# A hybrid block on one core: projection groups in another order (recurrent and gate groups in turn, the first v/z group and the gates moved forward)

## The chip, the core and the metric

The kernel runs on one core of one Trainium2 chip. The metric is the device time of one execution in microseconds. Times of instructions and waits come from one profiled execution.

## The reference

One layer of a decoder trunk with three parallel head groups. 2048 tokens of width 1024 are normalised and projected once to 5656 columns, whose parts feed attention, a Mamba-2 mixer (SSD) and a gated linear recurrence (RG-LRU); each branch has a SiLU gate, and the three are mapped back by one output projection and added to the input.

```python
u = rms_norm(h, norm_g[l])
proj = jnp.einsum('bsd,de->bse', u, w_in[l])
(q, k, v, z_att, f_raw, z_ssd, xbc, dt_raw, x_lru, z_lru) = jnp.split(proj, split_points, axis=-1)
log_f = jax.nn.log_sigmoid(f_raw + forget_b[l])
y_att = fox_attention(q, k, v, log_f, q_norm_g[l], k_norm_g[l]) * jax.nn.silu(z_att)
y_ssd = ssd_mixer(xbc, dt_raw, z_ssd, ...)     # silu(conv(xbc)), softplus(dt_raw + bias), chunked scan, y * silu(z_ssd), norm
y_lru = rglru_mixer(x_lru, ...) * jax.nn.silu(z_lru)   # conv, two 64-wide gate products per block, scan over time
mix = jnp.concatenate([y_att, y_ssd, y_lru], axis=-1)
h = h + jnp.einsum('bse,ed->bsd', mix, w_out[l])
```

The widths are 512 each for q, k, v, z_att, x_lru and z_lru, 1024 for z_ssd, 1536 for xbc, 8 for f_raw, 16 for dt_raw. All is float32.

## The kernel before, in words

**Projection.** The normalised input, transposed, stays in SBUF as two float32r parts, `uh` and `ul` (four token blocks `tb` of 512, eight slices `k` of 128 channels). Each projection of 256 columns is a *group*. `weights` (L178 to L196) gets a group's columns: for each of eight slices k one load (issued by SP) into a raw tile `wr` (4 buffers), a ScalarE cast to `wh` (L192), and a subtraction `wl = wr − wh` (L193) on the engines of `eng` in turn: VectorE, or GpSimd for even and VectorE for odd k. `wh` and `wl` have eight buffers each, so a group's tile k takes the place of the previous group's tile k. A product is three matmuls per k: wh·uh, wh·ul and wl·uh. `proj_ch` (L347) puts channels on the partitions (128x512 matmuls, 24 to a tile), `proj_tok` (L315) and `proj_tok2` (L325) put tokens there (128x280 and 128x256); all take their PSUM from three banks, `psj`.

**Order.** The program text sets the order of the groups, and the scheduler interleaves the steps of neighbours:

1. the norm of x, block by block, with transposes by PE (`pu`, L293/L295). x comes in 16 tiles `xt` from a pool of XB = 8 buffers;
2. six convolution groups (L409 to L446, tiles `pxx`, `accx`): convolution on ACT (L397, L402) and DVE (L405), tanh on ACT (L431) and a product on DVE (L432), transposes on PE (L439), stores to `xs_d`, `b_d`, `bt_d`, `ct_d`;
3. the first v/z group, `group_vz(0)` (L358, tiles `pvz`): 128 columns of v, 128 of z_att and the 24 of f_raw and dt_raw; its evictions are two DVE operations and two small copies (L387, L388) a tile;
4. four recurrent groups m = 0 to 3 (L523 to L615, tiles `pll` and `pzl`): each 128 columns of x_lru and 128 of z_lru, with the convolution, the gate products on PE (`pgal`, `pgxl`, L583 to L585), exponentials, tanh and Sqrt on ACT, the reciprocal (L591), a scan over time (L607) and the last product (L611) on DVE, and products for z on POOL (L567, L568). The steps' order is the string LORD;
5. four z groups for the SSD branch (L618 to L630, tiles `pzs`): a tanh on ACT into a tile `thzs`, one DVE operation into `zs`, a store. The first of them takes two of its eight tiles from the bank pool `pst`. `gates` (L453, decays of both branches: softplus, exponentials, cumulative sums by small matmuls) comes ahead of the second (GM = 1);
6. the SSD stage, in which the groups of q and k (`pqk`) and the other v/z groups fill TensorE, then attention and the output projection.

Engines run their own queues in program order, so an instruction that waits holds all behind it on its engine.

Of the kernel before, what the change touches and what calls it, by code (L numbers as in the profile page):

```python
# [8 lines left out]
F32 = mybir.dt.float32  # L9
# [3 lines left out]
AF = mybir.ActivationFunctionType  # L13
ALU = mybir.AluOpType
# [4 lines left out]
P = 128  # L19
S = 2048  # L20
D = 1024
NT = S // P
KD = D // P
EPS = 1e-6
C_Q, C_K, C_V, C_ZA, C_F, C_ZS, C_X, C_DT, C_XL, C_ZL = (
    0, 512, 1024, 1536, 2048, 2056, 3080, 4616, 4632, 5144)
# [12 lines left out]
NDV = 3  # L39
UP, DOWN = (0, 1, 2, 3, 4, 5, 6, 7), (7, 6, 5, 4, 3, 2, 1, 0)  # L40
ORD = (DOWN,) + (UP,) * 6 + (DOWN,)
XB = 8
GM = 1
PB = (2, 3, 2, 1)


# [1 line left out]
def hybrid_block(ctx, tc, x, norm_g, w_in, q_norm_g, k_norm_g, forget_b, ssd_conv_w, ssd_conv_b,  # L48
# [3 lines left out]
    def tpool(**kw):  # L52
        if kw.get("space") is not DRAM:
            kw["reuse_waits"] = "tile"
        return tc.tile_pool(**kw)

    V, A, G, T = nc.vector, nc.scalar, nc.gpsimd, nc.tensor
    dma = nc.sync.dma_start
# [16 lines left out]
    xs_d = [dram(f"xs_d{g}", [S, 512]) for g in range(2)]  # L75
    b_d = [dram(f"b_d{g}", [S, P]) for g in range(2)]
# [13 lines left out]
    ident = ctile("ident", [P, P])  # L90
# [14 lines left out]
    CV = {}  # L105
# [28 lines left out]
    def softplus(pool, y, xin, shape, tag):  # L134
        def tmp(nm):
            return pool.tile(shape, F32, name=f"{tag}_{nm}", tag=f"sp_{nm}")
        ax, e, d, z2, p = tmp("a"), tmp("e"), tmp("d"), tmp("z"), tmp("p")
        V.scalar_tensor_tensor(ax, xin, -1.0, xin, op0=ALU.mult, op1=ALU.max)
        A.activation(e, ax, AF.Tanh, scale=1.0 / 16.0)
        V.tensor_scalar(d, e, 1.0, None, op0=ALU.add)  # L140
        V.reciprocal(d, d)
        V.tensor_scalar(e, e, -1.0, 1.0, op0=ALU.mult, op1=ALU.add)
        V.tensor_tensor(e, e, d, op=ALU.mult)
        for _ in range(3):
            V.tensor_tensor(e, e, e, op=ALU.mult)
        V.tensor_scalar(d, e, 2.0, None, op0=ALU.add)
        V.reciprocal(d, d)
        V.tensor_tensor(e, e, d, op=ALU.mult)
        V.tensor_tensor(z2, e, e, op=ALU.mult)
        V.tensor_scalar(p, z2, 1.0 / 19.0, None, op0=ALU.mult)  # L150
        for k in (17, 15, 13, 11, 9, 7, 5, 3):
            V.scalar_tensor_tensor(p, p, 1.0 / k, z2, op0=ALU.add, op1=ALU.mult)
        V.scalar_tensor_tensor(p, p, 1.0, e, op0=ALU.add, op1=ALU.mult)
        V.tensor_scalar(ax, xin, 0.0, None, op0=ALU.max)
        V.scalar_tensor_tensor(y, p, 2.0, ax, op0=ALU.mult, op1=ALU.add)
# [22 lines left out]
    def weights(cols, rawp=wrp, eng=(V,)):  # L178

        n = sum(w for _, w in cols)  # L180
        i = gcount[0]
        gcount[0] += 1
        wh, wl = [], []
        for k in range(KD):
            raw = rawp.tile([P, n], F32, name=f"wr{i}_{k}", tag="wr")
            h = wp.tile([P, n], F32R, name=f"wh{i}_{k}", tag="wh")
            l = wp.tile([P, n], F32R, name=f"wl{i}_{k}", tag="wl")
            o = 0
            for c, w in cols:
                dma(raw[:, o:o + w], w_in[k * P:(k + 1) * P, c:c + w])  # L190
                o += w
            A.copy(h, raw)  # L192
            eng[k % len(eng)].tensor_tensor(l, raw, h.bitcast(F32), op=ALU.subtract)  # L193
            wh.append(h)
            wl.append(l)
        return wh, wl, n  # L196

    rtx = ExitStack()
    rtp = rtx.enter_context(tpool(name="rtp", bufs=2, side="right"))
    cvp = rtx.enter_context(tpool(name="cvp", bufs=2, side="right"))  # L200
# [146 lines left out]
    def proj_ch(w, m, tb, name):  # L347
        wh, wl, n = w
        ps = psj.tile([P, 512], F32, name=name, tag="pj")
        ms = slice(m * P, m * P + P)  # L350
        for k in range(KD):
            T.matmul(ps, wh[k][:, ms], uh[tb][k], start=(k == 0), stop=False)  # L352
            T.matmul(ps, wh[k][:, ms], ul[tb][k], start=False, stop=False)  # L353
            T.matmul(ps, wl[k][:, ms], uh[tb][k], start=False, stop=(k == KD - 1))  # L354
        return ps
# [39 lines left out]
    def conv(pool, ps, prev, wname, bname, m, nm, ntile, acc, tag=""):  # L395
        rt = pool.tile([P, 515], F32, name=f"rt{nm}", tag="rt" + tag)
        A.copy(rt[:, 3:515], ps)  # L397
        if prev is None:
            G.memset(rt[:, 0:3], 0.0)
        else:  # L400
            G.tensor_copy(rt[:, 0:3], prev[:, 512:515])
        A.activation(acc, rt[:, 3:515], AF.Identity, scale=c1(wname, 3 * ntile + m),  # L402
                     bias=c1(bname, m))
        for k in range(3):
            V.scalar_tensor_tensor(acc, rt[:, k:k + 512], c1(wname, k * ntile + m), acc,  # L405
                                   op0=ALU.mult, op1=ALU.add)
        return rt

    g0x = ExitStack()  # L409
    g0 = g0x.enter_context(tpool(name="g0", bufs=2))  # L410
    with tpool(name="cl", bufs=1) as cl:
        for gq in range(6):
            if gq == 3:
                ll = cl.tile([P, 4], F32, name="ll")
                j = CV["lam"]
                V.tensor_scalar(ll, cv[:, j:j + 4], -1.0, None, op0=ALU.mult)
                softplus(cl, lsp, ll, [P, 4], "spl")
                V.tensor_scalar(lsp, lsp, 8.0, None, op0=ALU.mult)
                V.tensor_scalar(nlsp, lsp, -1.0, None, op0=ALU.mult)
            w = weights([(C_X + gq * 256, 256)]) if gq else wx0  # L420
            prev = [None, None]
            for tb in range(4):
                for mm in range(2):
                    m = gq * 2 + mm
                    nm = f"x{m}_{tb}"
                    ps = proj_ch(w, mm, tb, f"px{nm}")
                    acc = cv3.tile([P, 512], F32, name=f"acc{nm}", tag="acc")
                    prev[mm] = conv(rtp, ps, prev[mm], "cw", "cb", m, nm, 12, acc, str(mm))

                    th = prev[mm][:, 0:512]  # L430
                    A.activation(th, acc, AF.Tanh)  # L431
                    V.scalar_tensor_tensor(acc, th, 1.0, acc, op0=ALU.add, op1=ALU.mult)  # L432
                    ts = slice(tb * 512, tb * 512 + 512)
                    if m >= 8:
                        dma((bt_d if m < 10 else ct_d)[m % 2][:, ts], acc)
                    if m < 10:
                        pt = pst.tile([P, 4, P], F32, name=f"ptx{nm}", tag="pt")
                        for i in range(4):
                            T.transpose(pt[:, i, :], acc[:, i * P:(i + 1) * P], ident)  # L439
                        st = cvp.tile([P, 4, P], F32, name=f"st{nm}", tag="stx")  # L440
                        A.copy(st, pt)
                        if m < 8:
                            dst = xs_d[m // 4][ts, (m % 4) * P:(m % 4 + 1) * P]
                        else:
                            dst = b_d[m - 8][ts, :]
                        dma(dst.rearrange("(i p) c -> p i c", p=P), st)  # L446

    rtx.close()
    sgx = ExitStack()
    sg = sgx.enter_context(tpool(name="sg", bufs=1, side="right"))  # L450
    nacs, eacs, dec = (sg.tile([P, NT, 16], F32, name=nm) for nm in ("nacs", "eacs", "dec"))

    def gates(g1):  # L453

        dtb = g1.tile([P, 16], F32, name="dtb")
# [60 lines left out]
        for t in range(NT):  # L516
            dma(c_d[:, t, :], cr[t * 8:(t + 1) * 8, :])

    group_vz(g0, g0, 0)
    g0x.close()  # L520


    with tpool(name="lxs", bufs=2) as lxs, tpool(name="lp1", bufs=1) as lp1, tpool(name="lp", bufs=2) as pool:  # L523
        wbd = {}
        HB = 1024
        for m in range(4):
# [86 lines left out]

            for st in LORD.split():
                {"x": stage_x, "z": stage_z, "g": stage_g}[st[0]](int(st[1]))  # L615


    with tpool(name="zp", bufs=2, side="right") as pool, tpool(name="g1", bufs=1, side="right") as g1:  # L618
        for gq in range(4):
            if gq == GM:  # L620
                gates(g1)
            w = weights([(C_ZS + gq * 256, 256)], eng=(G, V) if gq < 2 else (V,))
            for t2 in range(8):
                zt = pool.tile([P, 2, 256], F32, name=f"zs{gq}_{t2}", tag="zs")
                ps = proj_tok2(w, t2, f"pzs{gq}_{t2}", (pst, "pt") if t2 % 5 > 2 and gq == 0 else None)
                th = pool.tile([P, 2, 256], F32, name=f"thzs{gq}_{t2}", tag="thzs")
                A.activation(th, ps, AF.Tanh, scale=0.5)
                V.scalar_tensor_tensor(zt, th, 1.0, ps, op0=ALU.add, op1=ALU.mult)
                dst = zs_d[gq // 2][t2 * 256:(t2 + 1) * 256, (gq % 2) * 256:(gq % 2 + 1) * 256]
                dma(dst.rearrange("(i p) c -> p i c", p=P), zt)  # L630

    sx = ExitStack()
    s1 = sx.enter_context(tpool(name="s1", bufs=1, side="right"))
# [478 lines left out]
```

## Time and profile before

| | us |
|---|---|
| median of 3 runs (2066.79 to 2068.64) | 2068.15 |
| the profiled execution | 2066.93 |
| its span | 2065.2 |
| PE busy | 2000.1 |
| DVE busy | 1268.8 |
| ACT busy | 978.6 |
| POOL busy | 542.1 |

PE is TensorE's matmul, PEld its weight load, DVE VectorE, ACT ScalarE, POOL GpSimd, SP the queue that issues most DMAs. In a timeline a row is start, duration, engine, line, operation, output<-input, shape; in brackets stands how long the engine had been idle and what released it. A wait row has the engine and line that waited, what it waited for, the sum in us, how often, and the longest. Matmuls overlap: a 128x512 matmul is recorded as 0.39 us and the next starts 0.23 us behind it. The granted clock is TensorE's, as a share of full speed.

### The profile page before, as it was taken

To read this page: it belongs to the slowest core of one execution; us is meant where nothing else is said; L and a number is where in the kernel's file an instruction comes from. 1 tells how busy PE (TensorE), PEld (TensorE's weight loads), DVE (VectorE), ACT (ScalarE), POOL (GpSimd) and SP (SyncE) were. 2 spreads that over 40 slices of the span, in tenths; PEclk is the share of its full clock that TensorE was granted. 3 is DMA by queue.
4 is the path that set the end of the run, shared out by engine and by line. 5 is a ranking of instruction groups with operands and counts; after the bars stand their busy time and mean duration, and the time that the engine had idled before them with its cause. 6 is when DMAs were issued, how large, how long until landed. Compare 5 with 4: busy or idle time off the path is not lost. (4 is left out here: it accounts for less than half of the span.)

```text
span 2065.2 us, 36048 instructions
## 1 busy us (share of the span) xinstructions
PE 2000.1 (97%) x12517; PEld 1756.8 (85%) x12517; DVE 1268.8 (61%) x2684; ACT 978.6 (47%) x2049; POOL 542.1 (26%) x790
## 2 busy tenths in 40 slices
PE   7999999999999999989999999899998999999999
PEld 6788889887789999878888998788887888888887
DVE  6755553488885225768666255666776776875333
ACT  7644443466642114544444234566665666664110
POOL 0100000255531004455553001243333333323110
PEclk9999999999999999999999999999999999999999
DMA  5222232111123225657666746575476375443443
GB/s 195 59 72 67 77 98 81 44 43 43 42 62 103 69 75 152 200 174 211 200 165 181 194 128 200 145 194 160 135 192 171 112 189 163 121 131 89 137 142 118
DMA packets 287317, 265.18 MB, mean 128 GB/s; under 512 B 59780, under 2 KB 227232, under 8 KB 285088
## 3 DMA queue, kind: packets, MB, share of 16 engines
q1 hardware_dynamic: 286976, 262.85, 43.9%
q8 instruction: 99, 1.62, 0.3%
q0 software_dynamic: 160, 0.03, 0.1%
q14 instruction: 82, 0.67, 0.1%
HBM read 168.22 MB, written 94.57 MB: 127 GB/s over the span
## 5 line engine op out<-in xcount | busy, mean ns | idle before, releaser
L940 DVE TENSOR_TENSOR pl<-T,ph 128x512 fp32r<-128x512 f32 (+2 forms) x352 | 191.3, 565 | 71.7 <-ACT ph L939 70.2
L1002 PE MATMUL po<-woh,mh 128*128 128x512 f32 x512 | 213.0, 416 | 10.2 <-DVE xr L1010 5.3
L939 ACT CAST ph<-T 128x512 fp32r<-128x512 f32 (+2 forms) x352 | 161.9, 491 | 124.5 <-PE T L932 85.0
L1003 PE MATMUL po<-wol,mh 128*128 128x512 f32 x512 | 201.9, 394 | 0.0
L1004 PE MATMUL po<-woh,ml 128*128 128x512 f32 x512 | 200.8, 397 | 0.0
L932 PE MATMUL T<-ident,L 128*128 128x128 f32 x1088 | 171.6, 275 | 3.9 <-ACT L L882 2.8
L882 ACT ACTIVATE L<-L,mx 128x1920 f32<-128x1920 f32 (+15 forms) x128 | 154.5, 1208 | 41.1 <-DVE mx L879 36.7
L352 PE MATMUL pxx<-uh,wh 128*128 128x512 f32 x384 | 153.0, 402 | 3.4 <-ACT uh L297 3.4
L918 PE MATMUL O<-ph,vv 128*128 128x256 f32 x576 | 154.1, 288 | 0.6 <-ACT ph L939 0.5
L919 PE MATMUL O<-pl,vv 128*128 128x256 f32 x576 | 152.4, 289 | 0.4 <-DVE pl L940 0.3
L353 PE MATMUL pxx<-ul,wh 128*128 128x512 f32 x384 | 152.7, 401 | 0.0
L340 PE MATMUL pqk<-wh,ul 128*128 128x256 f32 x512 | 151.1, 295 | 0.0
L354 PE MATMUL pxx<-uh,wl 128*128 128x512 f32 x384 | 151.1, 396 | 0.0
L336 PE MATMUL pqk<-wh,uh 128*128 128x256 f32 x512 | 150.2, 294 | 0.0
L338 PE MATMUL pzs<-wl,uh 128*128 128x256 f32 x512 | 144.6, 283 | 2.8 <-POOL wl L193 2.8
L338 PE MATMUL pqk<-wl,uh 128*128 128x256 f32 x512 | 145.9, 285 | 0.0
L336 PE MATMUL pzs<-wh,uh 128*128 128x256 f32 x512 | 144.6, 283 | 0.7 <-ACT wh L192 0.7
L405 DVE SCALAR_TENSOR_TENSOR accx<-rtx,cv,accx 128x512 f32<-128x512 f32 x144 | 108.2, 752 | 59.9 <-ACT accx L402 56.3
L340 PE MATMUL pzs<-wh,ul 128*128 128x256 f32 x512 | 144.2, 282 | 0.0
L932 PEld LDWEIGHTS T<-ident,L 128*128 128x128 f32 x1088 | 126.8, 141 | 15.2 <-ACT L L882 6.8
L871 POOL TENSOR_SCALAR_AFFINE_SELECT cm<-cb 128x384 f32<-128x384 f32 (+3 forms) x128 | 58.8, 462 | 300.9 <-DVE mx L879 146.2
L670 ACT ACTIVATE ab<-ab,nacs 128x128 f32<-128x128 f32 x256 | 82.2, 391 | 117.3 <-POOL ab L666 117.1
(319 smaller groups left out, 5605.6 us busy)
## 6 DMA issues: line engine op xcount, KB each, us to landing
ab<-acs_d SPq DMA_DIRECT2D x64, 256.0 KB
pt_d<-xr SPq DMA_DIRECT2D x64, 256.0 KB
wr<-in_w_in_dram SPq DMA_DIRECT2D x192, 64.0 KB
wr<-in_w_in_dram SPq DMA_DIRECT2D x80, 128.0 KB
xt<-in_x_dram SPq DMA_DIRECT2D x16, 512.0 KB
xs_d<-stx SPq DMA_DIRECT2D x32, 256.0 KB
v_d<-vs SPq DMA_DIRECT2D x32, 256.0 KB
zs_d<-zs SPq DMA_DIRECT2D x32, 256.0 KB
```

What stands on the lines that cost most here:

```text
L336: T.matmul(ps[:, i, :], h[k][:, sl], wh[k], start=(k == 0 and i == 0), stop=False, skip_group_check=True)
L338: T.matmul(ps[:, i, :], h[k][:, sl], wl[k], start=False, stop=False, skip_group_check=True)
L340: ins = T.matmul(ps[:, i, :], l[k][:, sl], wh[k], start=False, stop=last, skip_group_check=True)
L352: T.matmul(ps, wh[k][:, ms], uh[tb][k], start=(k == 0), stop=False)
L882: A.activation(lt[:, 0:n], lt[:, 0:n], AF.Exp, bias=mx, scale=-1.0, accum_out=sm[:, i:i + 1])
L918: T.matmul(po[:, ca], vv[:, kt, :], ph[:, jj, ca], start=(kt == 0), stop=False)
L932: ins = T.transpose(pt[:, jj, i * P:(i + 1) * P], L[i][:, kt * P:(kt + 1) * P], ident)
L939: A.copy(ph[:, ja, ca], pt[:, ja, ca])
L940: V.tensor_tensor(pl[:, ja, ca], pt[:, ja, ca], ph[:, ja, ca].bitcast(F32), op=ALU.subtract)
L1002: T.matmul(ps, mh[:, j, :], h, start=(j == 0), stop=False)
L1003: T.matmul(ps, mh[:, j, :], l, start=False, stop=False)
L1004: T.matmul(ps, ml[:, j, :], h, start=False, stop=(j == 3))
```

## The change

The numbers are computed as before; the order of the groups is another, with what makes room for it:

- the pool of x tiles has 7 buffers instead of 8 (XB), the three tiles `nacs`, `eacs`, `dec` are allocated at the start, and `gates` gets its own tiles beside the convolutions;
- `group_vz(0)` is issued ahead of the second convolution group (gq = 1), `gates` ahead of the third (gq = 2);
- the z groups become a function `group_zs`, called behind each recurrent group, so that they run recurrent 0, z 0, recurrent 1, z 1, and so on. All four z groups split their `wl` between GpSimd and VectorE (before, the last two had VectorE alone), all tiles take their PSUM from `psj`, and the tanh is written into `zs` itself, in which DVE then works in place.

From the end of the last z group on, every engine has the same instructions in the same order.

```diff
-XB = 8
-GM = 1
+XB = 7
...
+    sgx = ExitStack()
+    sg = sgx.enter_context(tpool(name="sg", bufs=1, side="right"))
+    nacs, eacs, dec = (sg.tile([P, NT, 16], F32, name=nm) for nm in ("nacs", "eacs", "dec"))
...
-    with tpool(name="cl", bufs=1) as cl:
+    with tpool(name="cl", bufs=1) as cl, tpool(name="g1", bufs=1, side="right") as g1:
         for gq in range(6):
+            if gq == 1:
+                group_vz(g0, g0, 0)
+            if gq == 2:
+                gates(g1)
...
-    group_vz(g0, g0, 0)
     g0x.close()
+    zpx = ExitStack()
+    zp = zpx.enter_context(tpool(name="zp", bufs=2, side="right"))
+
+    def group_zs(gq):
+        w = weights([(C_ZS + gq * 256, 256)], eng=(G, V))
+        for t2 in range(8):
+            ps = proj_tok2(w, t2, f"pzs{gq}_{t2}")
+            zt = zp.tile([P, 2, 256], F32, name=f"zs{gq}_{t2}", tag="zs")
+            A.activation(zt, ps, AF.Tanh, scale=0.5)
+            V.scalar_tensor_tensor(zt, zt, 1.0, ps, op0=ALU.add, op1=ALU.mult)
+            dst = zs_d[gq // 2][t2 * 256:(t2 + 1) * 256, (gq % 2) * 256:(gq % 2 + 1) * 256]
+            dma(dst.rearrange("(i p) c -> p i c", p=P), zt)
...
             for st in LORD.split():
                 {"x": stage_x, "z": stage_z, "g": stage_g}[st[0]](int(st[1]))
...
-    with tpool(name="zp", bufs=2, side="right") as pool, tpool(name="g1", bufs=1, side="right") as g1:
-        for gq in range(4):
-            if gq == GM:
-                gates(g1)
-            w = weights([(C_ZS + gq * 256, 256)], eng=(G, V) if gq < 2 else (V,))
-            for t2 in range(8):
-                zt = pool.tile([P, 2, 256], F32, name=f"zs{gq}_{t2}", tag="zs")
-                ps = proj_tok2(w, t2, f"pzs{gq}_{t2}", (pst, "pt") if t2 % 5 > 2 and gq == 0 else None)
-                th = pool.tile([P, 2, 256], F32, name=f"thzs{gq}_{t2}", tag="thzs")
-                A.activation(th, ps, AF.Tanh, scale=0.5)
-                V.scalar_tensor_tensor(zt, th, 1.0, ps, op0=ALU.add, op1=ALU.mult)
-                dst = zs_d[gq // 2][t2 * 256:(t2 + 1) * 256, (gq % 2) * 256:(gq % 2 + 1) * 256]
-                dma(dst.rearrange("(i p) c -> p i c", p=P), zt)
+            if m < 3:
+                group_zs(m)
+    group_zs(3)
+    zpx.close()
```

On TensorE, the end of the first recurrent group (the last gate product, `pgxl0_2`) and what follows it; the numbers in a weight's name are the count of the group and the slice k. Before:

```order
L583 MATMUL pgxl0_2_4020<-xhl0_2_3853,bdhx0_3687 128x512
L584 MATMUL pgxl0_2_4020<-xhl0_2_3853,bdlx0_3688 128x512
L585 MATMUL pgxl0_2_4020<-xll0_2_3854,bdhx0_3687 128x512
L352 MATMUL pll1_0_4131<-uh0_0_147,wh8_0_4059 128x512
L353 MATMUL pll1_0_4131<-ul0_0_155,wh8_0_4059 128x512
L354 MATMUL pll1_0_4131<-uh0_0_147,wl8_0_4060 128x512
```

And in the changed kernel:

```order
L598 MATMUL pgxl0_2_4181<-xhl0_2_4014,bdhx0_3848 128x512
L599 MATMUL pgxl0_2_4181<-xhl0_2_4014,bdlx0_3849 128x512
L600 MATMUL pgxl0_2_4181<-xll0_2_4015,bdhx0_3848 128x512
L338 MATMUL pzs0_0_4267<-wh8_0_4220,uh0_0_147 128x256
L340 MATMUL pzs0_0_4267<-wl8_0_4221,uh0_0_147 128x256
L342 MATMUL pzs0_0_4267<-wh8_0_4220,ul0_0_155 128x256
```

The second recurrent group's first tile has given its place to the first z group's, which asks for its `wl` one matmul earlier.

On GpSimd, the end of the second recurrent group: the subtractions for the group that follows (`wl9` before, `wl10` in the changed kernel), the low part of the convolution's result (`xll`) and the products of the z columns (`tzl`, `ZZ`). Before:

```order
L193 TENSOR_TENSOR wl9_0_4495<-wr9_0_4493,wh9_0_4494 128x256
L554 TENSOR_TENSOR xll1_3_4382<-XC1_1_4255,xhl1_3_4381 128x512
L193 TENSOR_TENSOR wl9_2_4509<-wr9_2_4507,wh9_2_4508 128x256
L193 TENSOR_TENSOR wl9_4_4523<-wr9_4_4521,wh9_4_4522 128x256
L567 TENSOR_TENSOR tzl1_2_4411<-tzl1_2_4411,ZZ1_1_4385 128x512
L567 TENSOR_TENSOR tzl1_3_4441<-tzl1_3_4441,ZZ1_1_4385 128x512
L193 TENSOR_TENSOR wl9_6_4537<-wr9_6_4535,wh9_6_4536 128x256
L568 TENSOR_TENSOR ZZ1_1_4385<-tzl1_2_4411,ZZ1_1_4385 128x512
```

And in the changed kernel:

```order
L569 TENSOR_TENSOR xll1_3_5015<-XC1_1_4888,xhl1_3_5014 128x512
L192 TENSOR_TENSOR wl10_0_5128<-wr10_0_5126,wh10_0_5127 128x256
L192 TENSOR_TENSOR wl10_2_5140<-wr10_2_5138,wh10_2_5139 128x256
L192 TENSOR_TENSOR wl10_4_5152<-wr10_4_5150,wh10_4_5151 128x256
L192 TENSOR_TENSOR wl10_6_5164<-wr10_6_5162,wh10_6_5163 128x256
L582 TENSOR_TENSOR tzl1_2_5044<-tzl1_2_5044,ZZ1_1_5018 128x512
L582 TENSOR_TENSOR tzl1_3_5074<-tzl1_3_5074,ZZ1_1_5018 128x512
L583 TENSOR_TENSOR ZZ1_1_5018<-tzl1_2_5044,ZZ1_1_5018 128x512
```

The four subtractions stand together, behind `xll` and ahead of the z products; at the end of the first recurrent group they are mixed with them as before.

On SP, the loads of x behind the first weight tiles of the second group in the program's order (`wr1`: the second convolution group before, the v/z group with four pieces a tile in the changed kernel). Before:

```order
L239 DMA rows_298<-in_k_norm_g_dram 1x64
L240 DMA rows_298<-in_k_norm_g_dram 1x64
L190 DMA wr1_0_1041<-in_w_in_dram 128x256
L190 DMA wr1_1_1047<-in_w_in_dram 128x256
L208 DMA xt8_312<-in_x_dram 128x1024
L208 DMA xt9_314<-in_x_dram 128x1024
```

And in the changed kernel:

```order
L242 DMA rows_304<-in_k_norm_g_dram 1x64
L189 DMA wr1_0_1050<-in_w_in_dram 128x128 x2
L189 DMA wr1_0_1050<-in_w_in_dram 128x8
L210 DMA xt7_299<-in_x_dram 128x1024
L210 DMA xt8_318<-in_x_dram 128x1024
L210 DMA xt9_320<-in_x_dram 128x1024
```

The load of `xt7`, which before stood right behind `xt6`, now stands here, in front of `xt8`.

More of the change, by code (lines that the diff above doesn't have):

```diff
@@ L407, in conv @@
         return rt
-    g0x = ExitStack()
-    g0 = g0x.enter_context(tpool(name="g0", bufs=2))
-    with tpool(name="cl", bufs=1) as cl:
[L412 to L451, printed above, removed]
     def gates(g1):
@@ L517, in gates @@
             dma(c_d[:, t, :], cr[t * 8:(t + 1) * 8, :])
-    group_vz(g0, g0, 0)
-    g0x.close()
+    g0x = ExitStack()
+    g0 = g0x.enter_context(tpool(name="g0", bufs=2))
+    with tpool(name="cl", bufs=1) as cl, tpool(name="g1", bufs=1, side="right") as g1:
+        for gq in range(6):
+            if gq == 1:
+                group_vz(g0, g0, 0)
+            if gq == 2:
+                gates(g1)
+            if gq == 3:
+                ll = cl.tile([P, 4], F32, name="ll")
+                j = CV["lam"]
+                V.tensor_scalar(ll, cv[:, j:j + 4], -1.0, None, op0=ALU.mult)
+                softplus(cl, lsp, ll, [P, 4], "spl")
+                V.tensor_scalar(lsp, lsp, 8.0, None, op0=ALU.mult)
+                V.tensor_scalar(nlsp, lsp, -1.0, None, op0=ALU.mult)
+            w = weights([(C_X + gq * 256, 256)]) if gq else wx0
+            prev = [None, None]
+            for tb in range(4):
+                for mm in range(2):
+                    m = gq * 2 + mm
+                    nm = f"x{m}_{tb}"
+                    ps = proj_ch(w, mm, tb, f"px{nm}")
+                    acc = cv3.tile([P, 512], F32, name=f"acc{nm}", tag="acc")
+                    prev[mm] = conv(rtp, ps, prev[mm], "cw", "cb", m, nm, 12, acc, str(mm))
+                    th = prev[mm][:, 0:512]
+                    A.activation(th, acc, AF.Tanh)
+                    V.scalar_tensor_tensor(acc, th, 1.0, acc, op0=ALU.add, op1=ALU.mult)
+                    ts = slice(tb * 512, tb * 512 + 512)
+                    if m >= 8:
+                        dma((bt_d if m < 10 else ct_d)[m % 2][:, ts], acc)
+                    if m < 10:
+                        pt = pst.tile([P, 4, P], F32, name=f"ptx{nm}", tag="pt")
+                        for i in range(4):
+                            T.transpose(pt[:, i, :], acc[:, i * P:(i + 1) * P], ident)
+                        st = cvp.tile([P, 4, P], F32, name=f"st{nm}", tag="stx")
+                        A.copy(st, pt)
+                        if m < 8:
+                            dst = xs_d[m // 4][ts, (m % 4) * P:(m % 4 + 1) * P]
+                        else:
+                            dst = b_d[m - 8][ts, :]
+                        dma(dst.rearrange("(i p) c -> p i c", p=P), st)
```

1 line of the change is left out of this document (added).

## The prediction

> **What bounds the kernel now.** I read the page's busy shares first, then busy time by stretches of 50 us, then TensorE's waits. All times below are of the profiled execution: it took 2066.93 us, its span is 2065.2 us.
>
> ```profile
> PE 2000.1 (97%) x12517; PEld 1756.8 (85%) x12517; DVE 1268.8 (61%) x2684; ACT 978.6 (47%) x2049; POOL 542.1 (26%) x790
> ```
>
> ```profile
> 50.00:100.00 50.00, 48.23 (x253) 39.38 (x252) 39.43 (x94) 31.56 (x58) 5.50 (x15) 1.00 0.20 55
> 100.00:150.00 50.00, 50.00 (x239) 40.84 (x238) 29.67 (x45) 25.26 (x45) 1.31 (x8) 1.00 0.26 74
> 300.00:350.00 50.00, 48.86 (x302) 44.39 (x301) 23.36 (x60) 17.08 (x39) 0.60 (x4) 1.00 0.28 78
> 350.00:400.00 50.00, 50.00 (x298) 44.84 (x297) 17.35 (x45) 14.85 (x37) 9.08 (x11) 1.00 0.22 61
> 400.00:450.00 50.00, 50.00 (x218) 40.46 (x217) 43.01 (x41) 32.58 (x51) 24.09 (x23) 1.00 0.16 44
> 450.00:500.00 50.00, 47.49 (x203) 37.53 (x202) 43.18 (x40) 34.34 (x54) 27.22 (x26) 1.00 0.14 34
> 500.00:550.00 50.00, 47.99 (x199) 37.82 (x198) 43.27 (x38) 30.80 (x50) 25.98 (x25) 0.97 0.15 43
> 550.00:600.00 50.00, 46.42 (x244) 39.15 (x243) 42.19 (x36) 28.85 (x47) 22.83 (x16) 0.97 0.16 48
> 650.00:700.00 50.00, 50.00 (x426) 50.00 (x425) 9.30 (x17) 10.79 (x25) 4.34 (x5) 1.00 0.33 100
> ```
>
> The columns behind the stretch are PE, PEld, DVE, ACT, POOL, granted clock, DMA. PE is busy 97% of the span, so an order of groups can win only where PE pauses. From 450 to 600, the second to fourth recurrent group and the start of the z groups, it pauses; there DVE is busy 43 of 50, while under the z groups (650 on) it is busy 9. The waits say for whom:
>
> ```profile
> PE pll L354 <- POOL wl L193: 4.5, 4, 1.8
> PE pzs L338 <- POOL wl L193: 2.8, 3, 2.2
> PE pvz L320 <- DVE dt L388: 1.1, 1, 1.1
> PE pzs L336 <- ACT wh L192: 0.7, 2, 0.5
> ```
>
> All but pvz are waits of a group's first tile for its own weights, split into wh by ACT and wl by POOL: 8.0 us. The full price is larger. Starts of PE in the recurrent stage:
>
> ```profile
> 413.83 0.39 PE L354 MATMUL pzl<-uh,wl 128*128 128x512 f32 x1
> ...
> 421.71 0.39 PE L352 MATMUL pll<-uh,wh 128*128 128x512 f32 x1
> ```
>
> ```profile
> 579.21 0.39 PE L585 MATMUL pgxl<-xll,bdhx 128*128 128x512 f32 x1
> 579.83 0.38 PE L336 MATMUL pzs<-wh,uh 128*128 128x256 f32 x1 [0.23 <-ACT wh L192]
> 582.39 0.54 PE L338 MATMUL pzs<-wl,uh 128*128 128x256 f32 x1 [2.18 <-POOL wl L193]
> 582.73 0.42 PE L340 MATMUL pzs<-wh,ul 128*128 128x256 f32 x1
> ...
> 585.48 0.56 PE L338 MATMUL pzs<-wl,uh 128*128 128x256 f32 x1 [0.19 <-POOL wl L193]
> ...
> 585.99 0.28 PE L336 MATMUL pzs<-wh,uh 128*128 128x256 f32 x1
> 586.11 0.28 PE L338 MATMUL pzs<-wl,uh 128*128 128x256 f32 x1
> ```
>
> From 413.83 to 421.71 are 34 starts: 0.232 us each. A recurrent group is 192 + 24 of these, 50.1 us. At 421.71 the second group begins, with no wait; the fourth ends its place at 579.21 + 0.23 = 579.44. Three groups took 157.7 instead of 150.3: 7.4 lost. Into the z group, 15 narrow starts (0.12 each, as 585.99 to 586.11) and one wide one lie between 579.21 and 585.99: 2.0 us of work in 6.8, 4.8 lost; two later waits there (the sums leave 2.8 − 2.18 − 0.19 = 0.4 for wl and 0.7 − 0.23 = 0.5 for wh; with the refill about 0.75 each) make it 6.3. In all 13.7, against 8.0 of idle. The rest is slow matmuls behind the waits:
>
> ```profile
> 528.00:532.00 4.00, 3.83 (x10) 2.59 (x11) 3.52 (x5) 1.21 (x4) 3.76 (x3) 0.59 0.53 155
> 582.00:586.00 4.00, 3.41 (x15) 3.12 (x16) 4.00 (x5) 1.42 (x4) 4.00 (x4) 0.57 0.32 98
> ```
>
> The granted clock was 0.59 and 0.57 there, behind waits of 1.8 and 2.2 us. The Trainium skill, TensorE: Matmul & The Clock Gate, section "HAM oscillation — how this bites in real kernels", states the rule as no idle gaps over about 3.4 us; by it waits this short would leave the clock alone, and their removal would bring the idle alone. The rows show otherwise, so the measurement decides: I take 13.7.
>
> **Why the weights are late.** The ScalarE cast of the next group's first weight tile, ahead of the second recurrent group and ahead of the first z group:
>
> ```profile
> 416.03 0.40 ACT L192 CAST wh<-wr 128x256 fp32r<-128x256 f32 x1
> ...
> 579.38 0.40 ACT L192 CAST wh<-wr 128x256 fp32r<-128x256 f32 x1
> ```
>
> They are three groups and 163.35 apart, 54.4 each. So the recurrent chain on ACT, DVE and POOL needs 54.4 per group where PE needs 50.1. At the first boundary the cast came 5.7 ahead of PE (416.03 against 421.71) and nothing was lost; by the last it came 0.06 ahead. Four recurrent groups in a row use up the lead.
>
> **The change part by part.**
>
> *Recurrent and z groups alternate (−13.7, +1).* A z group is 384 starts of 0.12, 46 us of PE with 9 of 50 on DVE; it lets the chain's lag drain. So each recurrent group starts as the first did, from drained queues, and each of the four recurrent-to-z boundaries should look like 416 to 428, not like 579. The z tile asks for a weight tile every 6 x 0.12 = 0.72 us, the recurrent one every 3 x 0.232 = 0.70: the same pace. The four POOL subtractions:
>
> ```profile
> 416.51 2.50 POOL L193 TENSOR_TENSOR wl<-wr,wh 128x256 fp32r<-128x256 f32 x1 [8.88 <-ACT wh L192]
> ...
> 427.51 1.04 POOL L193 TENSOR_TENSOR wl<-wr,wh 128x256 fp32r<-128x256 f32 x1
> ```
>
> The last was ready at 428.55, 6.8 behind the boundary; a z tile beginning at 421.71 and giving way to three gate matmuls, as at 579, wants it at about 428.8. The slack is 0.2, so I allow 0 to 1 us per boundary, 1 in all. In the z groups of the second and later boundaries POOL's order puts the four subtractions ahead of the recurrent products, which brings them earlier. The z-to-recurrent boundaries find DVE idle and cost nothing, as the one behind the first v/z group (PE is busy 50.00 of 50 from 350 to 400, where the first recurrent group begins). The extra PSUM tile of the first z group goes; the first z eviction ran at
>
> ```profile
> 597.17 0.69 DVE L628 SCALAR_TENSOR_TENSOR zs<-thzs,pzs 128x512 f32<-128x512 f32 x1 [1.18 <-ACT thzs L627]
> ```
>
> 17.7 behind the boundary with a lag of 5.7, so about 12 without it; the fourth tile needs the first's bank at 3 x 48 x 0.12 = 17. Covered. The tanh written in place must wait for the store two tiles earlier, 11 us before: nothing.
>
> *First v/z group behind the first convolution group (−1.4, +1).* Its one wait (1.1 us idle, 1.4 with the refill) goes with its place. At the new place DVE has the first group's backlog: 39.43 of 50 busy from 50 to 100 against 23.36 in its place before, and the last product of that group ran long after PE had left it:
>
> ```profile
> 100.37 0.69 DVE L432 SCALAR_TENSOR_TENSOR accx<-rtx,accx 128x512 f32<-128x512 f32 x1 [0.78 <-ACT rtx L431]
> ```
>
> The fourth v/z tile needs the first's bank. That tile's evictions stand among the last products in DVE's order, where the backlog would reach them near 94.7, and PE asks near 94.5. Bounds: 0 (as all v/z tiles but one), and 6 (100.4 − 94.5, were it behind the whole backlog); I take 1, the nearest row's 1.1.
>
> *Gates under the second and third convolution group (+0.5).* Where they run now, DVE (the second number) did:
>
> ```profile
> 608.90:648.90 40.00, 32.82 (x104) 1.00 0.31 96
> ```
>
> Less eight z evictions of 0.69 that is at most 27.3 us for the gates, in a stage in which DVE had room, so nothing is gained there. They enter one where 29.67 of 50 are used (100 to 150): 57.0, so 7 too much, if all fell on one 50 us group; but the order spreads them over more than one, and PE's transposes stand a tile (24 x 0.232 = 5.6 us) behind the product that DVE makes for them. Bounds 0 and 7, I take 0.5.
>
> *Seven x buffers (+0.75).* The eighth x load now waits for the first x tile's release, and on SP for the first weight tile of the v/z group, as the ninth did. The eighth's and ninth's squares on ACT, the thirteenth's, and PE's transposes of the second block:
>
> ```profile
> 21.32 1.09 ACT L265 ACTIVATE sq<-xt 128x1024 bf16<-128x1024 f32 x1
> ...
> 26.78 1.06 ACT L265 ACTIVATE sq<-xt 128x1024 bf16<-128x1024 f32 x1 [2.82 <-DMA xt<-in_x_dram]
> ...
> 45.59 1.06 ACT L265 ACTIVATE sq<-xt 128x1024 bf16<-128x1024 f32 x1 [1.99 <-DMA xt<-in_x_dram]
> ```
>
> ```profile
> 31.03 2.35 PE L295 MATMUL pu<-ident,xt 128*128 128x128 f32 x20
> ```
>
> The eighth's square moves from 21.32 to 26.78, 4.2 ahead of those transposes (31.03); the square's 1.06 and some 3 us of scaling fit in about that. The twelfth takes the thirteenth's place, 45.59, ahead of the third block's scale on ACT; I estimate that block 0.75 later, the square's 1.06 less a little that ACT idles. Bounds 0 and 2.8, the ACT wait itself.
>
> Sum: 2066.9 − 13.7 − 1.4 + 1 + 1 + 0.5 + 0.75 = 2055.0. The median of the runs is 1.2 above the profiled execution, so a median could read 2056; I forecast **2055**. No change means within 0.2%, 4.1 us, about what a measurement of this kernel can tell.
>
> **The rivals.**
>
> *Slower: every recurrent-to-z boundary waits as the one at 579 (0.12).* POOL's subtraction depends on what DVE runs beside it:
>
> ```profile
> 579.85 2.49 POOL L193 TENSOR_TENSOR wl<-wr,wh 128x256 fp32r<-128x256 f32 x1 [10.17 <-ACT wh L192]
> ...
> 591.74 0.90 POOL L193 TENSOR_TENSOR wl<-wr,wh 128x256 fp32r<-128x256 f32 x1
> ```
>
> ```profile
> 579.54 2.28 DVE L607 TENSOR_TENSOR_SCAN MM<-RA,XC 128x1024 f32<-128x1024 f32 x1
> ...
> 592.09 3.35 DVE L591 RECIPROCAL RA<-RA 128x512 f32<-128x512 f32 x1
> ```
>
> Beside the scan it took 2.49, beside the reciprocal 0.90. The change gives POOL the wl of all four z groups, all under such tails. The Trainium skill, SBUF — State Buffer, section "SBUF: two separate sides", calls the port pair that DVE and GpSimd share an exclusive lock, which a DVE instruction with two SBUF inputs holds to its end; the two rows agree with it. Price 6.3 each, 25.2 in all, less the 1 allowed: 2079. It decides from a lead of the cast under about 3 us. Against it stands the first boundary, same tail, same 2.50, no loss.
>
> *Part of the gain (0.15).* The later weight tiles (sixth to eighth) come 1.75 us late at each of four boundaries: 7 instead of 1, 2061.
>
> *DVE crowded (0.10).* The gates fall on one convolution group, 7 instead of 0.5, and the v/z tile waits behind the whole backlog, 6 instead of 1: 2055 + 6.5 + 5 = 2066.5, no change. The order of the products speaks against both.
>
> *The slow stretches stay (0.04).* If the half-clock stretches have another cause than these waits, only idle goes: 13.7 − 8.0 = 5.7 less, 2060.7. That both begin right behind waits speaks against it. It is what the Trainium skill's rule on gaps, cited above, would give.
>
> **How the numbers follow.** The forecast's case has 0.59, its own range 2051 (no allowance used) to 2059. Faster by over 0.2% (under about 2064): 0.59 + 0.15 + 0.04 = 0.78, less 0.01 for edges; same 0.11; slower 0.12. The range 2050 to 2067 leaves out the slower rival and little else.
>
> **What would show it.** Right: no wait of pll or pzs for wl over 0.5 us; the cast some 5 us ahead of PE at all four boundaries; granted clock 1.00 from 400 to 800; the SSD stage begins some 12 us earlier. Wrong: granted clocks near 0.6 at recurrent-to-z boundaries, pvz waiting for DVE by several us near 95, PE idle for uh near 35 or 54 beyond the present waits, or a later stage that loses what this one gained.

## The result and the profile after

The changed kernel took 2054.83 us (median of 4 runs, 2051.31 to 2056.60) against 2068.39 (4 runs, 2066.79 to 2069.58): a ratio of 0.9932, 95% interval 0.9912 to 0.9952. That is 13.6 us faster; the forecast was 2055. Its profiled execution took 2056.60 us, with a span of 2054.9.

The first view is busy time by stretches of 50 us (columns as before: PE, PEld, DVE, ACT, POOL, granted clock, DMA share, GB/s), over the stage in which recurrent and z groups now alternate.

```profile
450.00:500.00 50.00, 50.00 (x303) 44.41 (x302) 17.08 (x21) 14.72 (x27) 8.67 (x11) 1.00 0.17 48
500.00:550.00 50.00, 50.00 (x338) 46.02 (x338) 34.43 (x34) 28.17 (x44) 18.33 (x19) 1.00 0.22 65
550.00:600.00 50.00, 50.00 (x285) 43.54 (x284) 19.70 (x23) 16.82 (x31) 12.00 (x14) 1.00 0.15 43
600.00:650.00 50.00, 50.00 (x357) 46.89 (x356) 32.29 (x32) 25.30 (x39) 14.76 (x16) 1.00 0.23 70
```

PE is full where it lost 2.5, 2.0 and 3.6 us in 50 before, the granted clock is 1.00, and DVE's 43 of 50 is spread to 17 to 34. PE's waits no longer name pll, pzs or pvz. Those left before the SSD stage are all of the start, these three the longest:

```profile
PE pu L295 <- DVE dg L270: 8.1, 1, 8.1
PE pxx L354 <- ACT uh L299: 2.1, 1, 2.1
PE pu L297 <- DVE xt L280: 1.1, 1, 1.1
```

The lead, which the prediction put at some 5 us at all four boundaries: ACT's first cast for each z group, and then PE's first matmul of the first two of these groups.

```profile
418.08 0.40 ACT L191 CAST wh<-wr 128x256 fp32r<-128x256 f32 x1
...
514.24 1.31 ACT L191 CAST wh<-wr 128x256 fp32r<-128x256 f32 x4
...
609.77 1.32 ACT L191 CAST wh<-wr 128x256 fp32r<-128x256 f32 x4
...
705.47 1.31 ACT L191 CAST wh<-wr 128x256 fp32r<-128x256 f32 x4
```

```profile
423.77 0.28 PE L338 MATMUL pzs<-wh,uh 128*128 128x256 f32 x1
...
519.29 0.28 PE L338 MATMUL pzs<-wh,uh 128*128 128x256 f32 x1
...
757.48 0.36 PE L338 MATMUL pqk<-wh,uh 128*128 128x256 f32 x1
```

The lead is 5.7 and 5.05; the other two z groups begin at 614.82 and 710.35, so 5.05 and 4.9. From the second on the casts are 95.5 to 95.7 apart, as PE's groups are (95.5): the lead no longer shrinks.

To compare kernels whose late stages differ from run to run, the time on PE is cut at four marks: the last transpose of the start, the first pll, the first pqk (757.48 above, 770.53 in the kernel before) and the first px of the output tail.

| us | before | after | difference |
|---|---|---|---|
| start, to the last pu | 73.9 | 75.4 | +1.5 |
| convolution and first v/z group (after: gates too) | 299.1 | 299.7 | +0.6 |
| recurrent and z groups (before: gates too) | 397.5 | 382.4 | −15.2 |
| SSD and attention | 1123.4 | 1126.1 | +2.7 |
| tail | 171.3 | 171.3 | 0.0 |

These two executions are 10.3 apart, 3.3 less than the medians. The runs below show which rows of the table hold.

### The profile page after: what moved, and what is told of

It reads as the page before. It is cut to its first block, busy times and chain, and to the rows that moved or that the text cites. A ratio compares the mean times of both kernels' runs of the same rounds, so it can differ in the third digit from the quotient of the medians.

```text
span 2054.9 us, 36001 instructions
## 1 busy us (share of the span) xinstructions
PE 1997.6 (97%) x12517; PEld 1756.5 (85%) x12517; DVE 1255.9 (61%) x2676; ACT 978.7 (48%) x2049; POOL 536.7 (26%) x798
## 5 line engine op out<-in xcount | busy, mean ns | idle before, releaser
L1006 PE MATMUL po<-woh,mh 128*128 128x512 f32 x512 | 213.2, 416 | 10.4 <-DVE xr L1014 6.6
L407 DVE SCALAR_TENSOR_TENSOR accx<-rtx,cv,accx 128x512 f32<-128x512 f32 x144 | 108.1, 752 | 57.4 <-ACT accx L404 54.4
```

The costliest lines, as they stand in the source:

```text
L1006: T.matmul(ps, mh[:, j, :], h, start=(j == 0), stop=False)
```

## The experiments

The theory at first: the chain of ACT, DVE and POOL through a recurrent group has a period of 54.4 us where PE needs 50.1, so the lead of the weights shrinks by 4.3 for each recurrent group that follows another; a z group gives it back. The rivals: the gain comes from the moved v/z group and gates, or POOL's subtractions beside DVE's scan make the weights late at any boundary.

The measured times of one kernel spread widely (before: 2059.9 to 2083.0 over 35 runs), so each verdict gives the median and the interval of the ratio, and rests on the length of the stage of recurrent and z groups, from the first pll to the first pqk. Each ratio is to runs of the kernel before that were measured beside it; their medians were 2065.98 to 2069.11. The stage comes from one profile of each kernel. It was 382.4, 382.5 and 382.7 in the three with the changed kernel's order of groups (after, e8, e7); the others were profiled once. The gates' matmuls are in it for the kernel before, for all that keep its place for them, and for e1.

| run | median, us | ratio to before (95%) | recurrent and z stage, us |
|---|---|---|---|
| before (profile) | 2068.39 | 1 | 397.5 |
| after | 2054.83 | 0.9932 (0.9912 to 0.9952) | 382.4 |
| e8, after again | 2053.96 | 0.9941 (0.9920 to 0.9963) | 382.5 |
| e1, alternation alone | 2062.35 | 0.9961 (0.9942 to 0.9980) | 383.7 |
| e2, moves alone | 2070.34 | 1.0010 (0.9993 to 1.0026) | 395.6 |
| e3, pairs | 2063.14 | 0.9976 (0.9956 to 0.9996) | 390.8 |
| e4, no table loads | 2065.19 | 0.9989 (0.9972 to 1.0005) | 393.8 |
| e5, no reciprocal | 2069.85 | 1.0013 (0.9998 to 1.0028) | 393.0 |
| e6, no z products | 2061.41 | 0.9965 (0.9951 to 0.9979) | 389.3 |
| e7, eight x buffers | 2147.67 | 1.0392 (1.0370 to 1.0413) | 382.7 |
| e9, before with two ZZ | 2077.37 | 1.0050 (1.0033 to 1.0067) | 402.6 |
| e10, after with two ZZ | 2060.05 | 0.9974 (0.9959 to 0.9989) | 386.1 |

### e1: the alternation alone

In the kernel before:

```diff
             for st in LORD.split():
                 {"x": stage_x, "z": stage_z, "g": stage_g}[st[0]](int(st[1]))
+            if m < 3:
+                group_zs(m)
+    with tpool(name="g1", bufs=1, side="right") as g1:
+        gates(g1)
+        group_zs(3)
```

> The kernel before with the alternation alone: eight x buffers, the first v/z group behind the last convolution group as before, a z group behind each recurrent group; the gates, which need the first v/z group and room in SBUF, stand ahead of the last z group. Theory (the chain of ACT, DVE and POOL needs 54.4 us per recurrent group where PE needs 50.1, and a z group lets it drain): the 13.7 us of late weights go, the 1.4 us wait of pvz stays, the start stays, so about 2054.7, or up to 5 us more if the SSD stage waits for the late gates; ACT's first cast 5 us ahead of PE at all four boundaries. Rival (the gain comes from moving the v/z group and the gates out of the stage in which DVE and POOL are busy): about 2067, with wl waits at the boundaries.

The stage is 383.7 us, within 1.3 of the changed kernel's and, with the gates in it as before, 13.8 shorter than before. No wait of pll or pzs is left: the alternation alone takes the whole gain of this stage. Of the time only half came, 2062.35. The gates are the likely reason. In this kernel PE's first matmul of the SSD chunks themselves is

```profile
787.83 0.38 PE L656 MATMUL cb<-ct,bt 128*128 128x128 f32 x2
```

31.5 us behind the first pqk (756.31), where the changed kernel has it 0.14 us ahead of its pqk (757.34 and 757.48). The q and k groups that fill PE's pauses in the SSD stage are spent meanwhile. SSD and attention took 1135.8 us in this profile, 9.7 more than after, but that alone proves little: in the ten profiles in which PE has this stretch in the order of before and after (all but e1 and e7) it took 1117.3 to 1138.3. The medians say more. Those of e1 and e8 are 8.4 apart; by the ratios it is 0.0020, some 4 us, with intervals that overlap. The expectation allowed 5. So the moves earn nothing by themselves (e2), and yet about half of the gain seems to need them: they get the gates out of the way of the SSD stage. No third place for the gates was tried.

### e2: the moves alone

In the changed kernel:

```diff
-            if m < 3:
-                group_zs(m)
-    group_zs(3)
+    for gq in range(4):
+        group_zs(gq)
```

> The changed kernel with the four z groups behind the four recurrent groups again: only the v/z group, the gates and the seven x buffers are left of the change. Theory: the waits of before come back, 7.4 us from the second to the fourth recurrent group and about 6.3 into the first z group, with granted clocks near 0.6 in a few stretches of 4 us behind them: 2054.8 + 13.7 = 2068.5. Rival (the moves make the gain): about 2055, no wl wait of pll or pzs.

The waits are back, and the time with them:

```profile
PE pll L356 <- POOL wl L192: 5.8, 4, 1.8
PE pzs L340 <- POOL wl L192: 3.8, 3, 2.2
PE pzs L338 <- ACT wh L191: 0.8, 2, 0.6
```

The stage is 13.2 longer than after, as expected (13.7), and the rival falls. So does another: the z groups' smaller edits (the tanh in place, the split of all `wl`, PSUM from `psj` alone) are in this kernel too and gain nothing without the alternation. One part of the expectation fell too: there is no slow clock. Behind the wait of 2.18 us into the z group (the same length as before) the rows read

```profile
584.00:588.00 4.00, 1.73 (x13) 1.53 (x13) 4.00 (x5) 0.97 (x3) 4.00 (x4) 1.00 0.25 66
```

The granted clock stayed at 1.00, PE idled 10.4 us instead of 8.0, and the stage lost as much. PE waits for the weights of each slice; at half clock it spends part of that time on slow matmuls, at full clock it idles.

### e3: recurrent and z groups in pairs

In the changed kernel:

```diff
-            if m < 3:
-                group_zs(m)
+            if m == 1:
+                group_zs(0)
+                group_zs(1)
+    group_zs(2)
     group_zs(3)
```

> The changed kernel with the groups in pairs: recurrent 0 and 1, z 0 and 1, recurrent 2 and 3, z 2 and 3. Theory (the lead of 5 us at the first boundary shrinks by 54.4 - 50.1 = 4.3 us for each recurrent group that follows another, and waits begin when it is gone): the lead is about 5 us at recurrent 0 to 1 and 2 to 3, about 1 us at 1 to z 0 and 3 to z 2, where PE waits for wl as it did at the second boundary of before, about 3.5 us each: 2054.8 + 7 = 2061.8. Rival (entering a z group from a recurrent group is what costs, 6.3 us, when the one before it was also recurrent): 2054.8 + 12.6 = 2067.4. Rival (any z group behind any number of recurrent groups drains it in time): 2054.8.

Both boundaries behind a second recurrent group wait, the others do not:

```profile
PE pzs L340 <- POOL wl L192: 4.2, 3, 1.4
...
PE pgal L598 <- ACT RA L604: 2.0, 1, 2.0
...
PE pzs L338 <- ACT wh L191: 0.5, 1, 0.5
```

The casts at the first two boundaries came at

```profile
415.41 0.40 ACT L191 CAST wh<-wr 128x256 fp32r<-128x256 f32 x1
```

```profile
469.82 0.40 ACT L191 CAST wh<-wr 128x256 fp32r<-128x256 f32 x1
```

and PE reached them at 421.09 and 471.17: leads of 5.7 and 1.35, a loss of 4.3 per recurrent group, the number that the theory gave. The stage is 8.4 longer than after (7 expected, 12.6 and 0 by the rivals). The wait of pgal, a gate product behind the second pair, is in the 8.4 too; the expectation did not name it.

### e4, e5 and e6: what makes the chain slow

Three kernels in the order of before, each with one engine's share of the recurrent group made smaller.

```diff
-                A.activation(mm, mm, AF.Sqrt)
+                A.activation(mm, mm, AF.Square)
```

> The kernel before, order unchanged, with the square root of the recurrent branch's input scale replaced by a square, so that 16 of ACT's 18 table loads go (four of 1.28 us in each recurrent group). Theory (the chain's period sets the waits): 54.4 - 5.1 = 49.3 us per group, below PE's 50.1, so the lead no longer shrinks and the waits of pll and pzs for wl go without any alternation: 2068.4 - 13.7 = 2054.7, at least under 2059 if DVE or POOL keep part of the chain long. Rival (POOL's subtraction of 2.5 us beside DVE's scan makes the weights late, not ACT): the waits stay, 2068.

The expectation failed. The waits have other releasers now, but most of them stay:

```profile
PE pzs L338 <- DVE hc L610: 2.1, 1, 2.1
PE pll L354 <- DVE hc L610: 1.6, 1, 1.6
PE pll L354 <- DVE wl L193: 1.5, 2, 0.9
PE pzs L338 <- DVE wl L193: 0.9, 1, 0.9
```

5.1 us less of ACT per group shortened the stage by 3.7 in all. The table loads stood in front of the casts, but only a part of the chain's period was theirs: DVE, behind the same scans, was late next.

```diff
-                V.reciprocal(ra[:, sl], ra[:, sl])
```

> The kernel before, order unchanged, with the reciprocal of the recurrence gate left out (four of 3.35 us on DVE in each recurrent group, 13.4 us). Theory, mended: the period of 54.4 us is DVE's (43 of 50 busy, the rest waits of its own chain), the table loads lay beside it; with 13.4 us less the period falls below PE's 50.1 and the waits for wl go although four recurrent groups follow one another: the stage from the first recurrent group to the SSD stage about 13 us shorter, 2069.1 - 13 = 2056. Rival (POOL's subtractions of 2.5 us are late by themselves): waits for wl stay, 2069.

This failed as well, and more plainly. Over the same stretch, DVE is down from 43 of 50, yet PE still pauses:

```profile
500.00:550.00 50.00, 48.41 (x200) 38.33 (x199) 32.61 (x36) 33.32 (x53) 23.18 (x25) 0.97 0.12 33
```

The stage is 4.5 shorter, for 13.4 us of DVE less in each of four groups. The period is not the load of one engine. Of the 4.5 the median shows nothing, and these runs give no reason for it. (In the profile, an execution 7.1 us above that median, SSD and attention took 1138.3 us, the longest of the ten profiles with that order.)

```diff
                     A.copy(zz, pz)
-                    G.tensor_tensor(t3, t3, zz, op=ALU.mult)
-                    G.tensor_tensor(zz, t3, zz, op=ALU.add)
```

> The kernel before, order unchanged, with POOL's two products per z tile left out (eight of about 1.4 us in each recurrent group; z is used without its sigmoid). Theory (DVE's period is long because its instructions with two inputs wait for POOL's: 1.23 becomes 2.15 for the last product, 0.74 becomes 0.93 for the convolution, 0.43 becomes 0.87 for the sum ahead of the reciprocal): 2 x 0.9 + 12 x 0.19 + 4 x 0.44 = 5.9 us less DVE per group, a period of 48.5, below 50.1, and the waits for wl go: 2056. Rival (the products are beside the chain and DVE's durations are its own): 2069, the DVE durations unchanged.

This went most of the way, though the time stayed above the 2056 expected: no wait of pll is left, one of pzs (and one of 1.9 us of a gate product behind it), and the stage is 8.2 shorter.

```profile
PE pzs L338 <- POOL wl L193: 0.7, 1, 0.7
```

The DVE groups from the second recurrent group to the first z group, here:

```profile
L405 DVE SCALAR_TENSOR_TENSOR XC<-rtl,cv,XC 128x512 f32<-128x512 f32 x36 | 29.7, 833 | 9.4 <-ACT XC L402 9.0
L605 DVE TENSOR_TENSOR_SCAN MM<-RA,XC 128x1024 f32<-128x1024 f32 x3 | 9.8, 3266 | 0.1
...
L609 DVE SCALAR_TENSOR_TENSOR ZZ<-MM,ZZ 128x1024 f32<-128x1024 f32 x5 | 7.0, 1404 | 0.0
```

and in the kernel before, with POOL's products beside them:

```profile
L405 DVE SCALAR_TENSOR_TENSOR XC<-rtl,cv,XC 128x512 f32<-128x512 f32 x36 | 33.6, 934 | 2.6 <-ACT XC L402 1.8
L611 DVE SCALAR_TENSOR_TENSOR ZZ<-MM,ZZ 128x1024 f32<-128x1024 f32 x6 | 12.9, 2155 | 0.0
...
L607 DVE TENSOR_TENSOR_SCAN MM<-RA,XC 128x1024 f32<-128x1024 f32 x2 | 4.6, 2282 | 0.0
```

The convolution took 833 ns instead of 934, the last product 1404 instead of 2155, with the same shapes; the scan, though, took 3266 instead of 2282. And in e5, where POOL kept its products, the first two were shorter still:

```profile
L405 DVE SCALAR_TENSOR_TENSOR XC<-rtl,cv,XC 128x512 f32<-128x512 f32 x36 | 28.1, 782 | 6.8 <-ACT XC L402 6.2
...
L610 DVE SCALAR_TENSOR_TENSOR ZZ<-MM,ZZ 128x1024 f32<-128x1024 f32 x6 | 7.3, 1210 | 0.0
```

So the same DVE instruction takes longer in one arrangement than in another, and not only by the z products. That part of the period is POOL and DVE lengthening each other is argued from these rows; the Trainium skill's lock on the port pair (SBUF — State Buffer, "SBUF: two separate sides") is in line with that. Leaving out the products also takes a step out of the chain and empties POOL's queue ahead of the subtractions, and e6 does not tell these apart.

The period itself can be read in all of these kernels as the prediction read it, from ACT's cast ahead of the second recurrent group to the one ahead of the first z group, three groups later (PE's own pauses are in it):

| us | first cast | last cast | per group | expected |
|---|---|---|---|---|
| before | 416.03 | 579.38 | 54.4 | |
| e4, no table loads | 415.31 | 573.70 | 52.8 | 49.3 |
| e5, no reciprocal | 416.49 | 572.93 | 52.1 | under 50.1 |
| e6, no z products | 414.48 | 569.96 | 51.8 | 48.5 |

Each edit took 1.6 to 2.6 us off the period, out of the 4.3 by which it exceeds PE's 50.1, in one profile each; none brings it below PE's.

### e7 and e8: the start, and the changed kernel again

```diff
-XB = 7
+XB = 8
...
-    sg = sgx.enter_context(tpool(name="sg", bufs=1, side="right"))
+    sg = sgx.enter_context(tpool(name="sg", bufs=1))
```

In e7 the pool `sg` is opened behind the start, on the left; in e8 nothing is edited.

> The changed kernel with eight x buffers: the three small tiles of the gates are allocated on the other side of SBUF once the x tiles are gone. Theory (the start costs 1.5 us, since the eighth load of x waits): the last transpose of the start near 73.8 instead of 75.4, 2053.3 against 2054.8. Rival (the start differs from run to run by more than that, and the eighth load's delay is hidden): no difference from the changed kernel that can be told.

> The changed kernel once more. If the 2.7 us that its SSD and attention stages were longer than those of before (1126.3 against 1123.6) belong to the change, they are there again; if they are the spread of these stages, another value comes. The stage from the first recurrent group to the SSD stage is 382.4 again, and the start shows how far it differs between runs of one kernel.

e8 gives 382.5 again for the stage, and 1122.6 for SSD and attention: the 2.7 us given back in the profile after were the spread of these stages. The starts are no longer apart either. With seven x buffers the last pu began at 75.4 and 73.1 (after, e8) and at 76.0, 72.8 and 72.3 (e2, e3, e10), with eight at 73.9 (before), 73.6, 73.8, 73.6, 72.9, 72.0 (e1, e4, e5, e6, e9) and 74.75 (e7). The means are 73.9 and 73.5. The mechanism is there, the eighth square waits (e8):

```profile
26.66 1.06 ACT L267 ACTIVATE sq<-xt 128x1024 bf16<-128x1024 f32 x1 [3.28 <-DMA xt<-in_x_dram]
```

but it costs less than two starts of one kernel differ. e7 itself answers nothing on its time: with this edit the scheduler ordered the SSD stage in another way, and that lost some 94 us. Which of the two did it, the eighth buffer or the other place of the small tiles, is not shown. Busy time from 760 to 1060 of e7, then of e8:

```profile
760.00:1060.00 300.00, 233.08 (x1195) 171.35 (x1194) 172.18 (x263) 129.16 (x370) 173.05 (x181) 0.82 0.58 172
```

```profile
760.00:1060.00 300.00, 285.19 (x2090) 253.53 (x2090) 201.38 (x344) 142.11 (x402) 154.78 (x158) 0.98 0.63 185
```

In e7 PE has 1195 matmuls there instead of 2090, at a granted clock of 0.82 instead of 0.98: the filling groups stand later in its order (no matmul of pqk from 800 to 1000).

### e9 and e10: a second buffer for ZZ

In the trace of before, the walk back from a late cast runs into ACT's wait for a store:

```profile
ACT ZZ L566 <- DMA lr_d<-ZZ: 18.4, 5, 5.5
```

```diff
-                    ZZ[hb] = lp1.tile([P, HB], F32, name=f"ZZ{m}_{hb}", tag="ZZ")
+                    ZZ[hb] = pool.tile([P, HB], F32, name=f"ZZ{m}_{hb}", tag="ZZ")
```

e9 makes this edit in the kernel before, e10 in the changed one.

> The kernel before, order unchanged, with two buffers instead of one for the recurrent branch's gate tile ZZ. In the trace of before ACT stands 18.4 us in five waits for the store of the previous ZZ, up to 5.5 us each, ahead of its copy into the next one (16.5 from 421 to 580, 5.5 per group). Theory, mended again (the period of 54.4 us is the round of one ZZ: copy, POOL's products, reciprocal, scan, last product, store, and ACT's queue stands behind it): with the second buffer the period falls to about 49, below PE's 50.1, and the waits for wl go without any alternation: the stage from the first recurrent group to the SSD stage 13 us shorter, about 2055. Rival (another wait takes its place, MM's single buffer or ACT's order): the waits for wl stay for half or more, above 2061.

> The changed kernel with two buffers for ZZ. Theory: alternation has already taken all that late weights cost, PE loses nothing from 100 to 750, so nothing is left for the second buffer: the same stage, 382.4 us, and the same time, 2054. Rival (the z stores still hold the recurrent groups up): a stage shorter than 382.

Both expectations failed, and the theory of the single buffer with them. ACT's wait is gone, and the stage is 5 us longer in e9 (402.6), 3.7 longer in e10 (386.1). In e9 the period, read as above, is 56.0 (casts at 414.63 and 582.74). In e10 PE idled 1.5 us from 400 to 750; where the rest of its 3.7 went these rows do not say. With a buffer free POOL's products of z no longer wait for that store and fall beside other work of DVE. The first of the two products of a tile, in e9 and then in before:

```profile
L567 POOL TENSOR_TENSOR tzl<-tzl,ZZ 128x512 f32<-128x512 f32 x12 | 24.8, 2065 | 14.0 <-ACT ZZ L566 14.0
```

```profile
L567 POOL TENSOR_TENSOR tzl<-tzl,ZZ 128x512 f32<-128x512 f32 x12 | 16.0, 1342 | 19.6 <-ACT ZZ L566 19.6
```

2065 ns instead of 1342, and DVE was busy for 143.4 us from the second recurrent to the first z group instead of 137.1. The ratio of e9, 1.0050, says slower, too. That the overlap is the cause is argued from these rows, not tested apart. No version here beats the changed kernel.

## Why the prediction was right, point by point

- **Alternation, −13.7 + 1.** Right. e1 gives the gain without the moves, e2 none without the alternation, and e3 takes 8.4 of it back with two recurrent groups in a row. Stage against stage with the gates at the same place (after against e2) it is 13.2. The allowance of 1 at the boundaries was not needed: PE waits at none of the four.
- **The split of the 13.7 into 8.0 of idle and 5.7 of slow clock.** The sum was right, the reading of the second part was wrong. I took the half-clock stretches as a price on top of the waits. e2 had no such stretch, idled 2.4 us more, and lost about the same (13.2, against 13.8 from before to e1). As far as these two executions show, the arrival of the weights sets the loss, however PE passes the time.
- **Why the weights are late.** The lag of 4.3 per group was right to a tenth (e3). What makes the period 54.4 stays open in part. Without ACT's table loads it is 52.8 (e4), without the reciprocal 52.1 (e5), without POOL's z products 51.8 (e6): each carries a share, none the whole 4.3, and the waits went furthest without the z products (8.2 of the stage). The single ZZ is not behind it (e9).
- **First v/z group moved, −1.4 + 1.** The wait went with its place. At the new place the tile's evictions got in between the last products of the convolution group, as its order says:

```profile
95.31 0.17 DVE L390 COPY dt<-pvz 128x16 f32<-128x16 f32 x1
...
98.71 0.69 DVE L505 SCALAR_TENSOR_TENSOR accx<-rtx,accx 128x512 f32<-128x512 f32 x1 [0.40 <-ACT rtx L504]
```

  The forecast had them near 94.7. They were done near 95.5, and the fourth tile's start slipped by 0.2 us or less. The 1 was not needed.
- **Gates, +0.5.** No wait came of them from 100 to 750. What the working missed is that their place matters for the SSD stage: at the end of the z groups they cost some 4 to 8 us by the medians (e1), so "nothing is gained there" held only for the place that they had.
- **Seven x buffers, +0.75.** Not to be told from nothing: 73.9 against 73.5 in the mean of five and seven starts that spread over 4.0 us.
- **The sum and the rivals.** The forecast took 11.9 off the profiled execution, the measured medians are 13.6 apart: the allowances of 3.25 were mostly not needed. That 2055 was met to 0.2 is luck, as the median of before stood 1.5 above the execution that the sum started from. The slower rival had its mechanism right, POOL's subtraction took 2.50 us beside the scan again (418.55 to 421.05 in the profile after), but a lead of 5 us covers it, as the first boundary of before had said. The bound for "no change" was too small for how far single runs of this kernel spread.

## What to carry to other kernels

When PE idles at the boundary between groups of one kind, measure the period of the feeding chain from one boundary to the next and compare it with PE's; if it is longer, put groups that load the chain little between them before trying to shorten the chain, which here gave back at most 8.2 of 13.7 us when work was taken off a single engine. Ask of every piece that has to make room who waits for it later: the gates showed no wait of PE where they moved, and cost some 4 to 8 us at the one other place that was tried.

## What the runs showed of the hardware

Waits of much the same length were followed by half the clock in one execution and not in another: behind 2.18 us the granted clock was 0.57 over 4 us in the kernel before and 1.00 in e2. In e9, behind waits of 2.2 and 2.0 us, it was

```profile
476.00:480.00 4.00, 4.00 (x14) 3.23 (x13) 2.04 (x3) 2.85 (x6) 3.92 (x4) 0.71 0.72 204
...
530.00:534.00 4.00, 4.00 (x12) 3.22 (x13) 2.00 (x3) 2.08 (x5) 4.00 (x4) 0.64 0.68 190
```

So the length of one gap doesn't decide it. The rule that the prediction took from the Trainium skill (TensorE: Matmul & The Clock Gate, "HAM oscillation — how this bites in real kernels") held in e2 and not in the kernel before or in e9, where the clock fell behind gaps of about 2 us; the measurement decides. What else it depends on, no run here shows. The loss was about the same with such stretches and without (before and e2), so they should not be priced by themselves where something else is late at the same time.
